# Gathers asked for two experts ahead in a two-layer hybrid trunk, with zero rows written later, products in PSUM, one more 2 KB slot and an earlier split of the last share

## The chip, the cores and the metric

The kernel runs on one core of one Trainium2 chip. Five engines work side by side, each through its own instruction stream: TensorE (PE, matmuls; PEld is its weight load), VectorE (DVE), ScalarE (ACT), GpSimd (POOL) and SyncE (SP). They wait for each other through semaphores. [...] The metric is device microseconds of the whole program; lower is better. SBUF, the on-chip memory, has 128 partitions; PSUM, where matmuls write, has eight banks of 2 KB for each partition.

## The reference

512 tokens of 1024 values pass two layers. Each layer is a mixer and then a mixture of experts, each with a residual and a layer norm:

```python
for layer in range(2):
    m = conv_mixer(x, ...) if layer == 0 else rglru_mixer(x, ...)
    x = layer_norm(ALPHA * x + m, ln1_g[layer], ln1_b[layer])
    f = moe(x, w_router, b_router, moe_w1[layer], moe_w3[layer], moe_w2[layer])
    x = layer_norm(ALPHA * x + f, ln2_g[layer], ln2_b[layer])

# moe: a router picks one group of four experts, and in it two of them, for each token
hb = silu(xb @ w1[e]) * (xb @ w3[e])     # xb: the tokens that chose expert e
y  = hb @ w2[e]                          # 1024 x 1024 weights, float32, 16 experts
out[token] += gate * y
```

The mixer of layer 0 is an input projection to 2560 columns, a causal convolution of 31 taps with GLU, norm and swish on one half, a gated short convolution on the other, and an output projection. That of layer 1 is a gated linear recurrence.

## The kernel before

**Precision.** A float32 product runs as three passes: a weight tile `raw` is split into `wh` (rounded to fp32r by ACT, line L137) and `wl` (the remainder, subtracted by DVE or POOL, L148). Experts with few tokens (places `SMALL` = 2, 5, 8, 11 and 13 of the 16) are packed as half rows and multiply `raw` directly (class `Small`, matmuls L226); the others are blocks of up to 128 tokens (class `Block`, matmuls L305, gate product L326).

**The weight stream.** Class `Stream` loads all weights in a fixed order through SP's queue (L121): 1 MB for an expert's tile and 12 tiles for an expert (four units each of w1, w3 and w2), 512 KB for a tile of the mixers. A load waits until a slot of the `V8` or `V` pool is free; `ws.lead` says how many tiles are split ahead of their use, `ws.cap` how much may be held.

**Layer 0's mixer.** `conv_mixer` goes through 20 column tiles of the projection (PE L596 to L599). ACT evicts each (L800), splits the next weight tile (L137) and makes taps (L767, L772); DVE does most of the convolution's taps (L761), POOL some of the rest (L773) and weight subtracts. At each tile a `hook(idx)` is called. At `idx` 3 it builds constants on POOL and makes the generator `dram_rows`, which then advances one step with every tile: a POOL memset of a tile `zero` (L1059) and ten DMAs on ACT's queue that write it to DRAM (one of 0.5 MB at L1064 and four of 1 MB at L1068 for each layer), where it is the starting value of the rows into which the experts' results are scattered and of the rows that padding gathers.

**Routing.** `route` (L1115) computes places on DVE with narrow tiles of the small pool; `by_place` (L1243) reorders by a masked product `perm` of 128x1024 in a `V` slot and a sum (L1248, L1249), twice in a layer. The first expert's matmuls stand beside it on PE.

**The experts.** `moe` (L1345) takes the 16 places in order. In iteration `e` (current expert `cur`, next `nxt`) POOL first gathers the rows of expert `e + 1` by an indirect DMA into the one buffer `rows` (`gather`, L1325). Then PE does w1 and w3 of `cur`, each in four units (0 to 3). After `w3(2)`, `nxt.rows_in(xe)` transposes the gathered rows on PE (L271), which reads the buffer; then come `w3(3)`, the transposes of the hidden values (L215 in a small expert), the first unit `w1(0)` of `nxt`, and w2 of `cur`. At the end of the iteration ACT evicts y, and POOL scatters it to DRAM with an indirect DMA (`scatter`, L1340). So POOL's queue holds the scatter of `e - 1` right in front of the gather of `e + 1`.

```python
xe = self.gather(slots[e + 1], e + 1 in SMALL, rows)   # start of iteration e
...
cur.w3(2)
nxt.rows_in(xe)
```

**The last expert.** Its y is not scattered. `share(h)` scales one half of it (DVE, L1493), `total_mm(t, h)` adds it to token tile t on PE (L1499), `total_half(t, h)` folds the result into the sum `az` (DVE, L1506, L1507).

Of the kernel before, what the change touches and what calls it, by code (L numbers as in the profile page):

```python
# [11 lines left out]
F32 = mybir.dt.float32  # L12
F32R = mybir.dt.float32r
BF = mybir.dt.bfloat16
I32 = mybir.dt.int32
AF = mybir.ActivationFunctionType
OP = mybir.AluOpType
AX = mybir.AxisListType

P = 128  # L20
T = 512
NT = T // P
D = 1024
KD = D // P
HALF = 512
E = 16
# [3 lines left out]
ALPHA = 4.0 ** 0.25  # L30
LRU_C = 8.0
NV = 21
NW = 11

# [1 line left out]
SMALL = (2, 5, 8, 11, 13)  # L38
# [309 lines left out]
class Trunk:  # L348
# [766 lines left out]
    def route(self, meanwhile):  # L1115
        nc, v = self.nc, self.nc.vector
        G4 = NT * NG

        def s(w, dt=F32):

            return self.S([P, G4, w], dt, f"rt{w}{'b' if dt == BF else ''}", bufs=2 if w == 2 or dt == BF else 4)

        def b(ap, n):
            return ap.broadcast_to([P, ap.shape[1], n])

        def tg(ap):
            return ap.rearrange("p (t g) o -> p t (g o)", g=NG)

        desc = self.desc[:, None, 0:EPG]
        lg = self.logit.rearrange("p t (g e) -> p (t g) e", g=NG)  # L1130

        l = s(2)
        v.tensor_reduce(l[:, :, 0:1], lg, axis=AX.X, op=OP.max)
        e1, e2, f, lm = s(4), s(4), s(4), s(4)
        v.tensor_tensor(e1, lg, b(l[:, :, 0:1], EPG), op=OP.is_equal)
        top = self.S([P, NT, 1], F32, "top", bufs=2)
        v.tensor_reduce(top, l[:, :, 0].rearrange("p (t g) -> p t g", g=NG), axis=AX.X, op=OP.max)
        v.tensor_tensor(f, e1, desc.broadcast_to([P, G4, EPG]), op=OP.mult)
        q1, q2 = s(1), s(1)
        v.tensor_reduce(q1, f, axis=AX.X, op=OP.max)  # L1140
        v.tensor_tensor(e1, f, b(q1, EPG), op=OP.is_equal)
        v.scalar_tensor_tensor(lm, e1, -1e30, lg, op0=OP.mult, op1=OP.add)
        v.tensor_reduce(l[:, :, 1:2], lm, axis=AX.X, op=OP.max)

        d, r = s(2), s(2)
        topb = top.broadcast_to([P, NT, NG])
        for i in range(2):
            v.tensor_tensor(tg(d[:, :, i:i + 1]), tg(l[:, :, i:i + 1]), topb, op=OP.subtract)
        nc.scalar.activation(d, d, AF.Tanh, scale=0.5)
        meanwhile()  # L1150
        v.tensor_tensor(e2, lm, b(l[:, :, 1:2], EPG), op=OP.is_equal)
        v.tensor_tensor(f, e2, desc.broadcast_to([P, G4, EPG]), op=OP.mult)
        v.tensor_scalar(r, d, -1.0, 1.0, op0=OP.mult, op1=OP.add)
        v.reciprocal(r, r)
        v.scalar_tensor_tensor(d, d, 1.0, r, op0=OP.add, op1=OP.mult)
        v.tensor_reduce(q2, f, axis=AX.X, op=OP.max)

        gs, ge = s(1), s(1)
        v.tensor_tensor(gs, d[:, :, 0:1], d[:, :, 1:2], op=OP.add)
        v.tensor_tensor(e2, f, b(q2, EPG), op=OP.is_equal)  # L1160
        gm = self.S([P, NT, 2], F32, "gm", bufs=2)
        v.tensor_reduce(gm[:, :, 0:1], tg(gs), axis=AX.X, op=OP.max)
        v.tensor_tensor(f, e1, e2, op=OP.add)
        v.tensor_tensor(tg(ge), tg(gs), gm[:, :, 0:1].broadcast_to([P, NT, NG]), op=OP.is_equal)
        v.tensor_tensor(tg(ge), tg(ge), self.desc[:, None, 0:NG].broadcast_to([P, NT, NG]), op=OP.mult)
        v.tensor_reduce(gm[:, :, 1:2], tg(ge), axis=AX.X, op=OP.max)
        v.tensor_tensor(tg(ge), tg(ge), gm[:, :, 1:2].broadcast_to([P, NT, NG]), op=OP.is_equal)
        ab = s(4, BF)
        v.tensor_tensor(ab, f, b(ge, EPG), op=OP.mult)
        ab = ab.rearrange("p (t g) e -> p t (g e)", g=NG)  # L1170

        ps = self.bank([P, 2, NT, E])
        nc.tensor.matmul(ps[:, 0], self.tri, ab, start=True, stop=False)
        for t in range(1, NT):
            nc.tensor.matmul(ps[:, 0, t:], self.ones, ab[:, 0:NT - t], start=False, stop=(t == NT - 1))
        for t in range(NT):
            nc.tensor.matmul(ps[:, 1, 0], self.ones, ab[:, t], start=(t == 0), stop=(t == NT - 1))
        self.pos = self.S([P, NT, E], F32, "pos", bufs=1)
        v.scalar_tensor_tensor(self.pos, ps[:, 0], 1.0, ab, op0=OP.add, op1=OP.mult)
        self.cnt_ps = ps  # L1180
        self.gate_parts = (e1, e2, d, gs, ge)
# [61 lines left out]
    def by_place(self, dst, src):  # L1243

        v = self.nc.vector
        n = [P, NT, E, E]
        w = self.V(n, F32, "perm")
        v.tensor_tensor(w, src[:, :, None].broadcast_to(n), self.sel[:, None].broadcast_to(n), op=OP.mult)  # L1248
        v.tensor_reduce(dst, w, axis=AX.X, op=OP.add)  # L1249

    def extra_blocks(self):

# [92 lines left out]
    def moe(self, layer, loaded):  # L1345

        nc, tc, ws = self.nc, self.tc, self.ws
        v = nc.vector
        slots, hot = {}, []
# [9 lines left out]
        rows = self.R("in", "xe")  # L1359
        nc.gpsimd.memset(rows, 0.0)  # L1360
        xe = self.gather((first[0][:, 0:1],), False, rows)
# [15 lines left out]
        slots[0], = self.slot_rows([hot0], [aux(0)], [False], first)  # L1377
        fill([1, 2, 3], hot)
        hot = []
        for e in range(E):  # L1380
            cur, last = nxt, e == E - 1
            if not last:
                xe = self.gather(slots[e + 1], e + 1 in SMALL, rows)
            if e < 12:
                q = e // 4 * 4 + 4 + 2 * (e % 4)
                if e % 4 < 2:
                    hot += [self.one_hot(self.pos[:, :, i], nc.gpsimd, i in SMALL) for i in (q, q + 1)]
                if e % 4 == 2:
                    q = e // 4 * 4 + 4
                    fill(list(range(q, q + 4)), hot)  # L1390
                    hot = []
            if e == E - 2:
                ws.cap = 16
            if e:
                cur.w1(1)
                cur.w1(2)
                if last:
                    self.base_begin()
                cur.w1(3)
            cur.w3(0)  # L1400
            if e == 1:
                self.extra_blocks()
            if e == 4:
                self.nextra = nc.values_load(self.ni[0:1, 0:1], min_val=0, max_val=32)
            cur.w3(1)
            cur.w3(2)
            if not last:
                nxt = Small(self, ws) if e + 1 in SMALL else Block(self, ws, 4 if e == E - 2 else 2)
                nxt.rows_in(xe)
            ws.later = []  # L1410
            cur.w3(3)
            cur.turn(0)
            ws.lows()
            if last:
                cur.turn(1)
            else:
                nxt.w1(0, ws.next(), lambda h: h or cur.turn(1))
                ws.ahead()
            cur.w2(0)
            if last:  # L1420
                loaded()
                self.base_sum(0)
            cur.w2(1)
            if e == E - 2:
                self.place_rows(slots[E - 1][0])
            if last:
                break
            cur.w2(2)
            cur.w2(3)
            self.scatter(cur.ys, slots.pop(e), cur.small, ROOM[e])  # L1430
            if e == E - 2:
                with tc.If(self.nextra > 0):  # L1432
                    it = self.S([P, 1], F32, "it", bufs=1)
                    nc.vector.memset(it, 0.0)
                    self.kept = {}
                    with tc.For_i(0, self.nextra, 1):
                        self.extra(layer, it)
                    self.kept = None
# [8 lines left out]
        for t in range(NT):  # L1447
            self.total_mm(t, 0)
        cur.w2(3)
        for t in range(NT):  # L1450
            self.total_half(t, 0)
        self.share(1, cur.ys[1], gate)
        for t in range(NT):
            self.total_mm(t, 1)
        ws.total, ws.open, ws.cap = False, False, 10
        ws.lead = 4
# [115 lines left out]
def build(ctx, tc, I, out, dbg=None, stop=None):  # L1572
# [43 lines left out]
    steps, rows = [], []  # L1616

    def hook(idx):
        if idx == 1:
            k.channel_params(*rows0, prm)  # L1620
        if idx == 2:
            ws.low(nc.gpsimd)
            ws.cap = 18
        if idx == 3:
            k.consts()
            rows.append(k.dram_rows())
        if rows:
            next(rows[0], None)
        if idx == 5:
            k.channel_params(*rows1, prm1)  # L1630
            steps.append(k.router_weights(prm1[:, :, 10:11], prm1[:, :, 12:13]))
            next(steps[0])
        if idx in (8, 10):
            next(steps[0])
            ws.lead = 3
        if idx == 12:
            ws.lead = 2
            ws.low(nc.gpsimd, nc.vector)
        if idx == 14:
            ws.cap = 10  # L1640
        if idx == 19:
            ws.lead = 0

    k.conv_mixer(xT, first, prm, hook)
    xT = None
    g1 = k.bcast_rows(I["ln1_g"][0], "g1")
# [146 lines left out]
```

## Time and profile before

| | us |
|---|---|
| median of 3 runs | 1580.95 (1580.26 to 1586.53) |
| the profiled execution, its own time | 1580.28 |
| its span, first to last instruction | 1578.4 |
| PE busy in the span | 1411.9 |
| DVE busy in the span | 1124.9 |
| ACT busy, POOL busy | 772.8, 425.2 |

All times of the rows below are in microseconds from the span's start unless marked ns. A row of a timeline gives start, duration, engine, line and operation, output tile and input tiles, and in brackets how long the engine sat idle before it and what released it. The engines' busy time is of instructions; a matmul's record ends by a model, later than the next one starts. The granted clock of TensorE is given as a share of full speed. The stages are: layer 0's mixer to about 190 us, its routing to about 240, its experts to about 740, layer 1's mixer to about 960, its routing to about 1017, its experts to about 1540.

### The profile page before, as it was taken

What the parts mean: (1) busy time and instruction counts of PE and PEld (TensorE: products, weight loads), DVE (VectorE), ACT (ScalarE), POOL (GpSimd) and SP (SyncE); (2) the same over time, 40 slices, a digit from 0 to 9 for tenths busy, and PEclk for the clock granted to TensorE, in tenths of its full rate; (3) what the DMA queues carried; (4) which work ended last, traced back from release to release, by engine and by line L of the source; (5) the groups of instructions that cost most, each with busy time, mean ns of one, the idle gap of its engine ahead of it and who ended that gap; (6) DMA issues with size and microseconds to landing.
All of it is one profiled execution on the core that took longest, in us unless ns stands there. A gap on an engine that the chain in (4) does not pass through costs nothing. (4 is left out here: it accounts for less than half of the span.)

```text
span 1578.4 us, 18166 instructions
## 1 busy us (share of the span) xinstructions
PE 1411.9 (89%) x6456; PEld 1031.1 (65%) x6456; DVE 1124.9 (71%) x1234; ACT 772.8 (49%) x718; POOL 425.2 (27%) x370
## 2 busy tenths in 40 slices
PE   8898969999899998999589798699998999989982
PEld 7686738567486674667477677484775847755761
DVE  6798688568384683558989987884855848644786
ACT  3543227357374573457455421363755637543751
POOL 3783114104201401002473311240051014100043
PEclk9999979999999999999789899799999999999996
DMA  9833747999999999978922258499999999999681
GB/s 283 334 134 107 269 188 300 386 417 380 410 392 392 422 390 418 395 290 323 269 82 84 102 196 310 151 364 403 397 397 417 386 408 399 393 419 399 249 327 53
DMA packets 120838, 490.71 MB, mean 311 GB/s; under 512 B 14079, under 2 KB 53503, under 8 KB 70565
## 3 DMA queue, kind: packets, MB, share of 16 engines
q1 hardware_dynamic: 102240, 437.29, 71.4%
q0 software_dynamic: 11808, 35.28, 5.7%
q10 hardware_dynamic: 6692, 16.91, 2.8%
q8 instruction: 53, 0.87, 0.2%
q14 instruction: 45, 0.36, 0.1%
HBM read 469.50 MB, written 29.62 MB: 316 GB/s over the span
## 5 line engine op out<-in xcount | busy, mean ns | idle before, releaser
L148 DVE TENSOR_TENSOR wl<-raw,wh 128x2048 fp32r<-128x2048 f32 (+2 forms) x310 | 628.2, 2069 | 239.5 <-ACT wh L137 226.1
L137 ACT ACTIVATE wh<-raw 128x2048 fp32r<-128x2048 f32 (+1 forms) x312 | 535.0, 1757 | 113.2 <-PE p L305 19.2
L305 PE MATMUL p<-wh,xe 128*128 128x512 f32 x1344 | 346.5, 395 | 0.8 <-PEq L1432 0.6
L305 PEld LDWEIGHTS p<-wh,xe 128*128 128x128 f32 x1344 | 247.9, 188 | 56.2 <-issue 7.0
L1340 POOL DMA_INDIRECT yd<-y,io x30 | 31.3, 1044 | 772.6 <-DVE wl L148 321.5
L305 PE MATMUL p<-wl,xe 128*128 128x512 f32 x672 | 187.3, 390 | 2.4 <-DVE wl L148 2.4
L226 PE MATMUL b<-raw,xs 128*64 128x512 f32 x640 | 154.2, 626 | 0.0
L305 PEld LDWEIGHTS p<-wl,xe 128*128 128x128 f32 x672 | 125.8, 188 | 31.2 <-DVE wl L148 4.1
L596 PE MATMUL b<-xT,wh 128*128 128x512 f32 (+1 forms) x320 | 120.3, 382 | 13.2 <-ACT wh L137 13.2
L1272 POOL TENSOR_SCALAR S<-c,posp 128x128 bf16<-128x128 bf16 x96 | 124.9, 1314 | 0.5
L597 PE MATMUL b<-xT,wh 128*128 128x512 f32 (+1 forms) x320 | 119.0, 378 | 2.7 <-DVE xT L421 2.7
L226 PEld LDWEIGHTS b<-raw,xs 128*64 128x64 f32 x640 | 44.4, 144 | 81.4 <-issue 78.7
L148 POOL TENSOR_TENSOR wl<-raw,wh 128x1024 fp32r<-128x1024 f32 x28 | 71.9, 2574 | 37.6 <-ACT wh L137 37.6
L596 PEld LDWEIGHTS b<-xT,wh 128*128 128x128 f32 x320 | 62.6, 196 | 26.0 <-ACT wh L137 15.8
L599 PE MATMUL b<-xT,wl 128*128 128x512 f32 (+1 forms) x320 | 72.9, 371 | 2.0 <-DVE wl L148 2.0
L271 PE MATMUL b<-c,xe 128*128 128x128 f32 x176 | 31.4, 334 | 45.5 <-DMA xe<-x1d,ii 45.5
L597 PEld LDWEIGHTS b<-xT,wh 128*128 128x128 f32 x320 | 62.6, 196 | 13.5 <-DVE xT L421 3.2
L226 PE MATMUL b<-raw,hts 128*64 128x512 f32 x320 | 70.9, 595 | 0.0
L418 ACT ACTIVATE xe<-b 128x512 fp32r<-128x512 f32 x40 | 22.6, 596 | 92.6 <-PE b L271 92.5
L599 PEld LDWEIGHTS b<-xT,wl 128*128 128x128 f32 x320 | 56.8, 191 | 12.4 <-DVE wl L148 2.5
L421 DVE TENSOR_TENSOR xe<-b,xe 128x512 fp32r<-128x512 f32 x40 | 26.5, 686 | 53.1 <-ACT xe L418 53.0
L271 PEld LDWEIGHTS b<-c,xe 128*128 128x128 f32 x176 | 27.1, 212 | 55.2 <-DMA xe<-x1d,ii 41.0
(309 smaller groups left out, 1961.2 us busy)
## 6 DMA issues: line engine op xcount, KB each, us to landing
raw<-in_moe_w_dram SPq DMA_DIRECT2D x384, 1024.0 KB, 9.9
raw<-in_even_w_in_dram SPq DMA_DIRECT2D x20, 512.0 KB, 8.0
yd<-zero ACTq DMA_DIRECT2D x8, 1024.0 KB, 8.2
ay<-yd POOLq DMA_DIRECT2D x8, 1024.0 KB, 15.4
raw<-in_odd_w_in_dram SPq DMA_DIRECT2D x16, 512.0 KB, 7.1
raw<-in_even_w_out_dram SPq DMA_DIRECT2D x8, 512.0 KB, 8.9
x1d<-z POOLq DMA_DIRECT2D x8, 512.0 KB, 6.2
az<-x1d POOLq DMA_DIRECT2D x8, 512.0 KB, 12.4
```

Of the source, the lines that this page charges most:

```text
L137: self.k.nc.scalar.activation(wh, raw, AF.Copy)
L148: self.lo[0].tensor_tensor(wl, raw, wh.bitcast(F32), op=OP.subtract)
L226: self.nc.tensor.matmul(ps[64 * h:64 * h + 64], stat[i], w[0][:, i, h * HALF:(h + 1) * HALF], start=(first and i == 0), stop=(last and i = ...
L271: self.nc.tensor.transpose(ps[:, q], v[:, q // step, q % step], self.k.ident)
L305: self.nc.tensor.matmul(pss[j], stat[i][a], q[:, i, j * HALF:(j + 1) * HALF], start=(first and i == 0 and a == 0 and q is wh), stop=(last ...
L418: self.nc.scalar.activation(hi, src, AF.Copy)
L421: self.nc.vector.tensor_tensor(lo, src, hi.bitcast(F32), op=OP.subtract)
L596: nc.tensor.matmul(ps, ah, bh, start=(i == 0), stop=False)
L597: nc.tensor.matmul(ps, ah, bl, start=False, stop=False)
L599: nc.tensor.matmul(ps, al, bh, start=False, stop=(i == n - 1))
L1272: (eng or self.nc.vector).tensor_scalar(S[:, t], self.iota2 if small else self.iota, pos[:, t:t + 1], None, op0=OP.is_equal)
L1340: nc.gpsimd.indirect_dma_start(out=self.by_half(self.yd) if small else self.yd[:, :], out_offset=bass.IndirectOffsetOnAxis(ap=slot[2], axi ...
```

## The change

There are five edits. The gather of expert 1 is issued before the loop, and within iteration `e` the gather of expert `e + 2` right after `rows_in` of expert `e + 1`, so it stands in POOL's queue ahead of the scatter of `e`. `by_place` makes its product in two halves of 128x512 in PSUM banks, where it used one 128x1024 tile of SBUF. The generator of zero rows first advances at column tile index 10, so its memset and ten DMAs fall to indices 10 to 19. The pool of 2 KB slots has 12 where it had 11, and the narrow tiles of `route` are cut from one of them. At the end of the experts, `share(1)` comes after the first two `total_half`, and the other two alternate with their `total_mm`.

```diff
-NW = 11
+NW = 12
@@ route
+        cols, at = self.W([P, HALF], F32, "rt"), [0]
         def s(w, dt=F32):
-            return self.S([P, G4, w], dt, f"rt{w}{'b' if dt == BF else ''}", bufs=2 if w == 2 or dt == BF else 4)
+            if dt == BF:
+                return self.S([P, G4, w], dt, "rtb", bufs=1)
+            at[0] += G4 * w
+            return cols[:, at[0] - G4 * w:at[0]].rearrange("p (n w) -> p n w", w=w)
@@ by_place
-        n = [P, NT, E, E]
-        w = self.V(n, F32, "perm")
-        v.tensor_tensor(w, src[:, :, None].broadcast_to(n), self.sel[:, None].broadcast_to(n), op=OP.mult)
-        v.tensor_reduce(dst, w, axis=AX.X, op=OP.add)
+        n = [P, NT // 2, E, E]
+        for c in (slice(0, NT // 2), slice(NT // 2, NT)):
+            w = self.bank().rearrange("p (t q e) -> p t q e", t=NT // 2, q=E)
+            v.tensor_tensor(w, src[:, c, None].broadcast_to(n), self.sel[:, None].broadcast_to(n), op=OP.mult)
+            v.tensor_reduce(dst[:, c], w, axis=AX.X, op=OP.add)
@@ moe
+        xe = self.gather(slots[1], 1 in SMALL, rows)
         for e in range(E):
             cur, last = nxt, e == E - 1
-            if not last:
-                xe = self.gather(slots[e + 1], e + 1 in SMALL, rows)
...
                 nxt.rows_in(xe)
+                if e + 2 < E:
+                    xe = self.gather(slots[e + 2], e + 2 in SMALL, rows)
...
-        for t in range(NT):
+        for t in range(2):
             self.total_half(t, 0)
         self.share(1, cur.ys[1], gate)
-        for t in range(NT):
+        for t in range(2):
+            self.total_mm(t, 1)
+        for t in range(2, NT):
+            self.total_half(t, 0)
             self.total_mm(t, 1)
@@ hook
-        if rows:
+        if rows and idx >= 10:
             next(rows[0], None)
```

## Rows read from the trace of the kernel before

**Rows 1.** The page's head: the span, the busy time of each engine with its share of the span and its instructions, and the granted clock of TensorE in 40 equal slices, in tenths of full speed.

```profile
span 1578.4 us, 18166 instructions
PE 1411.9 (89%) x6456; PEld 1031.1 (65%) x6456; DVE 1124.9 (71%) x1234; ACT 772.8 (49%) x718; POOL 425.2 (27%) x370
PEclk9999979999999999999789899799999999999996
```

**Rows 2.** The waits of PE in 240 to 740 us (layer 0's experts, the first row) and in 1030 to 1540 us (layer 1's, the second row): total us, times, longest.

```profile
PE b L271 <- DMA xe<-x1d,ii: 16.3, 5, 4.1
...
PE b L271 <- DMA xe<-x1d,ii: 15.9, 5, 3.7
```

**Rows 3.** The timeline of PE around two small experts of layer 0: expert 2 (the first four rows) and expert 13 (the last four). Each begins with the six units w1(1) to w3(2) as one run of 48 matmuls.

```profile
301.16 10.52 PE L226 MATMUL b<-raw,xs 128*64 128x512 f32 x48
315.04 1.98 PE L271 MATMUL b<-c,xe 128*128 128x128 f32 x8 [3.36 <-DMA xe<-x1d,ii]
...
320.26 0.75 PE L215 MATMUL b<-c,hs 128*128 128x128 f32 x4 [0.80 <-DVE hs L245]
320.76 1.17 PE L305 MATMUL p<-wh,xe 128*128 128x512 f32 x4
...
661.09 10.52 PE L226 MATMUL b<-raw,xs 128*64 128x512 f32 x48
674.53 1.22 PE L271 MATMUL b<-c,xe 128*128 128x128 f32 x8 [2.92 <-DMA xe<-x1d,ii]
...
678.41 0.75 PE L215 MATMUL b<-c,hs 128*128 128x128 f32 x4 [0.79 <-DVE hs L245]
678.91 1.17 PE L305 MATMUL p<-wh,xe 128*128 128x512 f32 x4
```

**Rows 4.** Windows: their bounds and length, then busy time (instructions) of PE, PEld, DVE, ACT and POOL, the granted clock, the DMA share and GB/s. The first two rows and the sum are of ten windows, one for each small expert of both layers, from the end of its run of 48 matmuls to the first matmul of the next expert. The row behind the sum is the part of expert 13's window from the start of its transposes.

```profile
311.68:320.76 9.08, 4.92 (x21) 2.77 (x21) 2.07 (x3) 1.20 (x2) 0.00 (x0) 0.81 1.02 423
...
671.60:678.91 7.31, 3.60 (x21) 2.02 (x21) 1.98 (x3) 1.08 (x2) 0.00 (x0) 1.00 1.02 425
...
sum 88.37, PE 48.13 PEld 24.67 DVE 20.53 ACT 11.73 POOL 0.17; mean PE 4.81 PEld 2.47 DVE 2.05 ACT 1.17 POOL 0.02
...
674.53:678.91 4.38, 3.59 (x20) 2.02 (x21) 1.98 (x3) 1.08 (x2) 0.00 (x0) 1.00 1.02 425
```

**Rows 5.** The timeline of POOL at the start of expert 2, and the gathers among the DMA issues (count, median us from issue to landing).

```profile
302.20 1.07 POOL L1340 DMA_INDIRECT yd<-y,io  x1 [20.26 <-ACT y L1338]
303.57 1.05 POOL L1325 DMA_INDIRECT xe<-x1d,ii  x1 [0.31 <-issue]
...
xe<-x1d,ii POOLq DMA_INDIRECT x32, 9.2
```

**Rows 6.** The waits of SP's weight queue in 240 to 740 us (total, times, longest), and windows, with the columns of rows 4, over the blocks and small experts of layer 0, of layer 1, and of one stretch of blocks alone.

```profile
SPq L121 <- DVE wl L148: 193.5, 71, 20.3
SPq L121 <- PE p L305: 90.6, 51, 7.8
...
300.00:690.00 390.00, 369.67 (x1705) 247.17 (x1704) 233.50 (x176) 206.68 (x167) 65.40 (x57) 0.98 1.00 403
1078.00:1470.00 392.00, 372.09 (x1713) 248.53 (x1712) 233.95 (x177) 208.64 (x168) 67.05 (x58) 0.98 0.99 403
330.00:390.00 60.00, 60.00 (x275) 48.12 (x272) 48.52 (x32) 43.00 (x34) 17.91 (x12) 1.00 0.99 396
```

**Rows 7.** Layer 0's mixer: timelines of ACT (three rows), POOL and PE, a wait of DVE in 24 to 215 us (total, times, longest), and windows with the columns of rows 4.

```profile
41.41 1.06 ACT L137 ACTIVATE wh<-raw 128x1024 fp32r<-128x1024 f32 x1 [14.24 <-DMA raw<-in_even_w_out_dram]
...
57.41 1.06 ACT L137 ACTIVATE wh<-raw 128x1024 fp32r<-128x1024 f32 x1 [9.50 <-DMA raw<-in_even_w_in_dram]
...
124.24 0.70 ACT L772 ACTIVATE ctmp<-av,c 128x485 f32<-128x485 f32 x1 [8.19 <-DVE by L813]
...
37.68 2.06 POOL L1059 MEMSET zero<- 128x2048 f32 x1
...
58.52 0.63 PE L596 MATMUL b<-xT,wh 128*128 128x512 f32 x1 [4.84 <-ACT wh L137]
...
DVE av L801 <- ACT av L800: 9.0, 2, 5.9
...
60.00:145.00 85.00, 78.06 (x335) 63.53 (x335) 83.05 (x112) 36.78 (x51) 62.91 (x39) 0.97 0.46 169
20.00:60.00 40.00, 34.30 (x170) 28.64 (x169) 24.76 (x45) 9.95 (x14) 17.16 (x45) 0.98 1.09 337
75.00:135.00 60.00, 53.06 (x227) 42.91 (x225) 58.98 (x77) 23.59 (x33) 46.02 (x29) 0.97 0.26 92
```

**Rows 8.** The two operations of `by_place` (min, median and max ns, first and last start), the gate product of a block from PSUM (count, busy us and mean ns, then idle time before it), and the timeline of DVE behind the first routing.

```profile
L1248 DVE TENSOR_TENSOR perm<-pos,sel x2: 1224/1225/1226, 220.4 to 997.3; 128x1024 f32<-128x1024 f32 x2
L1249 DVE TENSOR_REDUCE posp<-perm x2: 1220/1220/1220, 221.6 to 998.5; 128x64 f32<-128x1024 f32 x2
...
L326 DVE TENSOR_TENSOR hs<-hs,p 128x512 f32<-128x512 f32 x44 | 30.2, 686 | 38.1 <-PE p L305 38.0
...
239.28 0.16 DVE L1307 TENSOR_REDUCE sg<-b 128x1 f32<-128x3 f32 x1 [2.27 <-PE b L1286]
```

**Rows 9.** The timeline of DVE at the second half of the last share, in layer 0 and in layer 1.

```profile
770.79 0.69 DVE L1506 TENSOR_TENSOR az<-az,b 128x512 f32<-128x512 f32 x1 [0.59 <-PE b L1499]
...
1550.24 0.69 DVE L1506 TENSOR_TENSOR az<-az,b 128x512 f32<-128x512 f32 x1 [0.60 <-PE b L1499]
```

## The prediction

> **What bounds the kernel now.** The first view is the page's head: PE is busy for 1411.9 of 1578.4 us, DVE for 1124.9, and the granted clock is at full speed in most slices [rows 1]. So PE is the first suspect, but the share is a mean over stages, and what counts is what ends PE's waits in each. The second view is therefore PE's waits in the two expert stages, which fill about 1000 us. One line stands out: PE waits for the gathered rows at L271, 16.3 us in five waits in layer 0 and 15.9 us in five in layer 1 [rows 2]. The third view, PE's timeline, tells where these five are. Expert 2, a small one, begins with a run of 48 matmuls that lasts 10.52 us; then PE stands still for 3.36 us until its successor's rows have landed, and the eight transposes that follow take 1.98 us where those of expert 13 take 1.22 [rows 3]. The windows give the reason: in expert 2's stretch the granted clock is 0.81, in expert 13's it is 1.00 [rows 4]. The reader is to see that the wait costs more than its own length where the clock falls to its lower level, 1.2 GHz, behind the standstill.
>
> Why is the gather late? On POOL it is issued at 303.57, behind the scatter at 302.20, so 2.4 us after expert 2's first matmul at 301.16, and a gather takes 9.2 us to land [rows 3, 5]. That sum is more than the 10.52 us of work in front of the transposes. A block has more work there, and only small experts show the wait.
>
> The second candidate in the expert stages is the weight stream: 403 GB/s over both layers' stretches with a DMA share of 0.99 to 1.00 [rows 6]. But its queue on SP waits for slots, 193.5 us for those that DVE frees and 90.6 us for PE's, up to 20.3 us at a time [rows 6]. A queue that waits for slots is ahead of its users; PE has no wait for a weight of that size [rows 2]. So PE bounds these stages, and 60 us of blocks run without a gap [rows 6].
>
> In layer 0's mixer it is different. From 60 to 145 us DVE is busy for 83.05 of 85 us, PE for 78.06 [rows 7]: DVE is the bound there. Ahead of it ACT is held twice, 14.24 us until 41.41 and 9.50 us until 57.41. ACT's queue has the DMAs of zero rows in it, the first of which needs the memset that POOL makes only at 37.68; and with the zero rows the DMA engines are full (share 1.09 in 20 to 60 us) [rows 7]. DVE waits 9.0 us for ACT's evictions in two waits, and PE 4.84 us in one [rows 7].
>
> **Part 1, the gathers.** Nothing is added: the same gathers, one place earlier. Issued when the transposes of e + 1 have read the buffer, the gather of e + 2 has the rest of expert e (w3(3), w1(0) of the next and w2) and six units of expert e + 1 in front of its use. The six units alone last 10.52 us even in a small expert, and a landing takes 9.2 [rows 3, 5]. So all ten waits go. What POOL now waits for, the transposes, is over before the scatter of e behind it has its input: the scatter in the timeline waited 20.26 us for ACT's y [rows 5]. Nothing else that PE needs soon stands there, so I cost that at 0.
>
> The saving: the ten windows from the end of a run of 48 to the next expert's first matmul sum to 88.37 us [rows 4]. With rows present such a window is what expert 13's is from its transposes on, 4.38 us at clock 1.00 [rows 4]. Ten are 43.8, so 44.6 us go. That leaves out that a matmul's record ends after its successor starts: the four transposes at 320.26 end at 321.01, the next matmul starts at 320.76, 0.25 us earlier [rows 3]. Ten such overlaps are 2.5 us. I take 44.6 + 2.5 = 47, with 44.6 and 49.5 (twice the overlap) as bounds if the rows are there. The transposes of the hidden values still wait 0.8 us each for DVE [rows 3]; that is what is late next.
>
> Can the weights follow? Each layer's stretch of 390 us must become 23.5 shorter, which asks for 403 x 390 / 366.5 = 429 GB/s if nothing is drawn from what is held. In the stalls the stream ran at 423 to 425 [rows 4]. At 425 the stretch can be 390 x (1 - 403/425) = 20.2 us shorter by rate alone; the other 3.3 us must come from weights held ahead, and the waits for slots of up to 20.3 us [rows 6] say they are there. I take no loss. The Trainium skill (DMA: Bandwidth & Descriptors, Specifications) gives about 358 GB/s as the limit of HBM for one core, which would make the weights the bound already and the gathers' removal worth nothing: about 1572 us. Here the stream holds 403 GB/s over 390 us and 425 in a window, so the trace does not agree, and I follow the trace.
>
> **Part 2, `by_place` in PSUM.** Removed are a product of 1.22 us and a sum of 1.22 us for each call, added two of each on half the size. A row with a PSUM operand of 128x512 is the gate product, 0.69 us [rows 8]: 4 x 0.69 = 2.76 against 2.44, so +0.3 a call, +0.6 a routing, +1.3 in all. Behind the calls DVE sits idle for 2.27 us until PE is done [rows 8], which covers 0.6. I take 0; uncovered it is +1.3. The freed 8 KB slot lets weight loads start earlier, which is worth nothing while weights are ahead.
>
> **Part 3, the zero rows later.** The same memset and ten DMAs, from the eleventh column tile on. What goes is ACT's wait at 41 us for the memset and its wait in 48 to 57 us in a full DMA system. On DVE, the later bound, that is the 9.0 us it waited [rows 7]. What comes: the memset of 2.06 us now stands in a POOL that is busy for 46.02 of 60 us (75 to 135), and ACT waits for it with its DMA; the transfers themselves fall where the DMA share is 0.26 [rows 7], so they collide with little. Bounds: 0, if ACT is held there as long as it was; 9.0 + 2.06 = 11, if the memset also slowed others and no longer does. I take 9.0 - 2.06 = 7.
>
> **Part 4, a twelfth slot, `route`'s columns in one.** No instruction is added. ACT was held once for 8.19 us by such a slot [rows 7], in the stretch where DVE is the bound; I take 0, at most 5.
>
> **Part 5, the last share.** `share(1)` earlier lets PE's second half start while DVE does the first tiles; DVE's waits for PE of 0.59 and 0.60 us [rows 9] go: 1.2 us. Lower bound 0, if the scaling only delays the sums by as much.
>
> **Sum.** 47 + 7 + 1.2 = 55.2. The profiled execution took 1580.3 us, 1.9 more than its span, which stays; the median of the runs is 0.7 above it. 1580.3 - 55.2 = 1525.
>
> **Rivals.** *The weight stream becomes the bound* (0.12): for it speaks a DMA share of 1.00 [rows 6], against it the waits for slots. If it can't exceed its mean rate, parts 3 and 5 remain, 1580.3 - 8.2 = 1572; with 425 GB/s and no stock, 2 x 20.2 replace the 47, 1532. Its middle is 1552. *ACT is held at the eleventh tile as it was at the fourth* (0.10): the busy POOL speaks for it, the light DMA against it; 1580.3 - 48.2 = 1532. *The gathers come no earlier* (0.05), since POOL is held by something that the trace of before doesn't show at that place: 1572. *Slower* (0.05): without its ten rests PE is granted a lower clock in the experts. PE is busy there for 369.67 + 372.09 = 742 us at a mean clock of 0.98 [rows 6]; at clock c they become 742 x 0.98/c. That eats the 55.2 and 7.9 more at c = 0.90; at 0.85 it is +111 and the time 1636. Against it: 60 us without a gap at clock 1.00 [rows 6]; the lower clock came behind rests [rows 4]. The Trainium skill (TensorE: Matmul & The Clock Gate, Part 1) knows a reduced clock under load once three cores of a die are busy and says that one core never trips it; the trace, with one core, agrees as far as its 60 us at 1.00 go.
>
> **Numbers.** The forecast has 0.68. Its own range: 44.6 alone gives 1536, 49.5 + 11 + 1.2 + 5 gives 1514. The range of 8 in 10 takes in half of the weight stream's case, 1512 to 1550. A measurement of this kernel can tell about 0.5%, 7.9 us, from no change. Faster: the forecast, the held ACT, and the first rival and the third but for their parts at 1572, together 0.90. Within 0.5%: these parts, 0.05. Slower: 0.05.
>
> **What would show it.** Right: no wait of PE at L271 for the gathered rows in either expert stage, a window of 4 to 4.5 us at clock 1.00 in each small expert, and a stretch of about 366 us at over 420 GB/s with few waits for weights; ACT without its holds at 41 and 57 us; DVE's wait for PE gone in the last share. Wrong: waits of PE or DVE for a raw weight or for `wl` in the later experts (first rival); ACT idle for over 5 us around 75 to 100 us in front of its DMA (second); a gather issued on POOL well behind the transposes (third); a granted clock under 0.95 in a stretch without rests (last).

## The result and the profile after

The changed kernel takes 1525.98 us, the median of three runs (1523.43 to 1530.19), and the ratio to the kernel before is 0.9646 (95% interval 0.9598 to 0.9694). Forecast was 1525 us. The profile shown is of the slowest of the three, 1530.19 us; a second one, of a later run with a span of 1524.2 us, stands beside it where the two differ.

The page's head, the lines that answer to [rows 1]:

```profile
span 1528.4 us, 18167 instructions
PE 1396.3 (91%) x6456; PEld 1026.4 (67%) x6456; DVE 1126.9 (74%) x1242; ACT 772.2 (51%) x718; POOL 432.9 (28%) x370
PEclk9999979999999999999799999799999999999995
```

PE has the same 6456 matmuls, and its busy time is 15.6 us less. About 13 of these lie in the ten windows of [rows 4], where eight had a granted clock of 0.80 to 0.83: records got shorter since fewer of them ran at the lower clock. The eight more instructions of DVE are the halves of `by_place`.

The waits of PE in layer 0's experts, 235 to 715 us, all that the trace shows, and the three largest of layer 1's, 980 to 1490 us (total, times, longest), answering to [rows 2]:

```profile
PE b L215 <- DVE hs L245: 4.0, 5, 0.9
PE p L305 <- DVE wl L148: 0.9, 2, 0.5
PE p L305 <- PEq L1439: 0.8, 1, 0.8
...
PE b L1509 <- DVE yl L1503: 5.5, 1, 5.5
PE b L215 <- DVE hs L245: 4.0, 5, 0.9
PE p L305 <- DVE wl L148: 2.5, 2, 1.9
```

The wait at L271 for gathered rows is gone from both. In the whole trace two such waits are left, 13.9 us, for the first expert's rows in the routing; these two stood before as well, with 13.3 us. PE's timeline around expert 2, answering to [rows 3], and POOL's around the same expert, answering to [rows 5]:

```profile
292.54 10.52 PE L226 MATMUL b<-raw,xs 128*64 128x512 f32 x48
302.99 1.23 PE L271 MATMUL b<-c,xe 128*128 128x128 f32 x8
304.14 1.94 PE L226 MATMUL b<-raw,xs 128*64 128x512 f32 x8
306.87 0.74 PE L215 MATMUL b<-c,hs 128*128 128x128 f32 x4 [0.79 <-DVE hs L245]
```

```profile
274.72 2.01 POOL L1331 DMA_INDIRECT xe<-x1d,ii  x1 [1.44 <-PE b L215]
293.57 1.01 POOL L1346 DMA_INDIRECT yd<-y,io  x1 [16.84 <-DVE su L1303]
304.49 1.01 POOL L1331 DMA_INDIRECT xe<-x1d,ii  x1 [9.91 <-PE b L271]
318.41 1.03 POOL L1346 DMA_INDIRECT yd<-y,io  x1 [12.91 <-DVE wl L148]
```

The gather for expert 3's rows is issued at 274.72, 28.3 us ahead of the transposes at 302.99. The next one follows at 304.49, right behind these, and the scatter stands behind it. The eight transposes take 1.23 us, not 1.98: PE no longer rests in front of them.

Windows, with the columns of [rows 4]: nine of the ten stretches between a small expert's run of 48 and the next expert's first matmul (of the tenth the trace shows no single run), first and last and the sum; then the expert stretches, which answer to [rows 6], and the start, which answers to [rows 7]:

```profile
303.06:307.37 4.31, 3.52 (x20) 1.95 (x21) 1.98 (x3) 1.08 (x2) 1.01 (x1) 1.00 1.02 430
...
1398.75:1403.06 4.31, 3.52 (x20) 1.95 (x21) 1.98 (x3) 1.08 (x2) 1.02 (x1) 1.00 1.01 420
sum 38.89, PE 31.70 PEld 17.55 DVE 17.78 ACT 9.77 POOL 9.44; mean PE 3.52 PEld 1.95 DVE 1.98 ACT 1.09 POOL 1.05
```

```profile
291.00:657.00 366.00, 361.98 (x1700) 244.13 (x1700) 231.70 (x176) 205.29 (x165) 66.08 (x56) 1.00 1.01 418
1046.00:1413.00 367.00, 362.97 (x1703) 244.36 (x1701) 232.41 (x176) 205.29 (x165) 66.05 (x56) 1.00 1.01 418
...
20.00:60.00 40.00, 40.00 (x199) 33.90 (x198) 33.71 (x59) 16.11 (x22) 23.80 (x50) 1.00 1.07 314
60.00:135.00 75.00, 70.51 (x303) 57.59 (x303) 71.81 (x96) 31.61 (x43) 56.48 (x34) 0.95 0.45 167
```

A stretch now lasts 38.89 / 9 = 4.32 us where it lasted 8.84 [rows 4]. Over a whole stretch of experts the clock is 1.00, and the DMA engines move 418 GB/s, where they moved 403 [rows 6]. This is all traffic: in 291 to 657 us 152.99 MB, of which SP's weight queue has 146.15 and the gathers and scatters 6.53.

Where the 50.0 us between the two profiled spans went, by PE's stage marks (end of the last matmul of layer 0's projection; first and last block matmul of each expert stage; end):

```
                                before    after   second profile of after
layer 0's projection             140.7    130.9    131.5
routing, first expert             98.7    100.0    101.0
layer 0's experts                527.4    504.7    504.4
share, layer 1's mixer, routing  250.6    250.3    249.9
layer 1's experts                527.7    510.2    504.8
last share, norm                  33.3     32.2     32.7
```

Layer 0's mixer and the two expert stages hold all of it; the 5 us between the two profiles of the changed kernel lie in the last expert of layer 1.

### The profile page after: what moved, and what is told of

Read it like the earlier page. It is cut to its first block, busy times and chain, and to the rows that moved or that the text cites. A ratio compares the mean times of both kernels' runs of the same rounds, so it can differ in the third digit from the quotient of the medians.

```text
span 1528.4 us, 18167 instructions
## 1 busy us (share of the span) xinstructions
PE 1396.3 (91%) x6456; PEld 1026.4 (67%) x6456; DVE 1126.9 (74%) x1242; ACT 772.2 (51%) x718; POOL 432.9 (28%) x370
## 5 line engine op out<-in xcount | busy, mean ns | idle before, releaser
L226 PE MATMUL b<-raw,xs 128*64 128x512 f32 x640 | 146.2, 598 | 0.0
L1331 POOL DMA_INDIRECT xe<-x1d,ii x32 | 37.3, 1167 | 291.9 <-PE b L271 138.4
L1344 ACT ACTIVATE y<-p,sg 128x512 f32<-128x512 f32 x40 | 25.3, 685 | 75.4 <-PE p L305 75.4
L761 DVE SCALAR_TENSOR_TENSOR b<-av,c,b 128x510 f32<-128x510 f32 (+27 forms) x87 | 59.8, 731 | 2.2 <-ACT b L754 1.3
L326 DVE TENSOR_TENSOR hs<-hs,p 128x512 f32<-128x512 f32 x44 | 30.2, 685 | 39.6 <-PE p L305 39.6
```

The costliest lines, as they stand in the source:

```text
L226: self.nc.tensor.matmul(ps[64 * h:64 * h + 64], stat[i], w[0][:, i, h * HALF:(h + 1) * HALF], start=(first and i == 0), stop=(last and i = ...
L326: self.nc.vector.tensor_tensor(self.hm[h], self.hm[h], self.p3[h], op=OP.mult)
L761: nc.vector.scalar_tensor_tensor(o[:, s:], av[:, 0:T - s], prm[:, i, 30 - s:31 - s], acc[:, s:], op0=OP.mult, op1=OP.add)
L1331: self.nc.gpsimd.indirect_dma_start(out=xe, out_offset=None, in_=self.by_half(self.x1d) if small else self.x1d[:, :], in_offset=bass.Indir ...
```

## The experiments

Each ratio is to the kernel before on the same chip. The experiments ran on three chips, so small differences from the changed kernel are judged by the ratios; its own, run again, is 0.9665 (0.9644 to 0.9686).

**The changed kernel again.**

> The changed kernel itself, so that what is compared with it has its time from the same chip. All theories expect about 0.965 of the kernel before, 1526 us, and the stage times of its first profile within 2 us: about 131 us for the end of layer 0's projection, 508 and 514 us for the two expert stages.

Measured: 1525.95 us (1525.35 to 1530.88, five runs). The projection ends at 131.5 us and the expert stages take 504.4 and 504.8 us. The total is as expected. Counted to the end of the last share, as the expectation did, the stages are 507.8 and 508.7 us: layer 1's is 5 us shorter than expected from the first profile. That is a spread between executions of the same kernel, and it lies in that stage's last expert.

**The gathers back.** Theory against a rival that gives the gain to the slots.

```diff
-        xe = self.gather(slots[1], 1 in SMALL, rows)
         for e in range(E):
             cur, last = nxt, e == E - 1
+            if not last:
+                xe = self.gather(slots[e + 1], e + 1 in SMALL, rows)
...
-                if e + 2 < E:
-                    xe = self.gather(slots[e + 2], e + 2 in SMALL, rows)
```

> The changed kernel with the gather of expert e + 1 issued at the start of iteration e again; the other four edits stay. My theory: the ten waits at L271 come back with their half clock, 47 us, so about 1573 us, and the expert stages are 23 us longer each. Rival, that the gain in the experts came from the freed slots and the twelfth 2 KB slot through the weight stream: 1526 us to 1535 us, with the expert stages as short as in the changed kernel.

Measured: 1568.82 us, ratio 0.9931 (0.9911 to 0.9951), 42.9 us above the changed kernel. Its expert stages take 526.2 and 527.4 us. The waits of PE in layer 0's experts and the timeline at expert 2:

```profile
PE b L271 <- DMA xe<-x1d,ii: 15.9, 5, 3.5
...
305.03 1.98 PE L271 MATMUL b<-c,xe 128*128 128x128 f32 x8 [3.51 <-DMA xe<-x1d,ii]
306.94 2.74 PE L226 MATMUL b<-raw,xs 128*64 128x512 f32 x8
```

All of it is back, and the eight transposes take 1.98 us again. With the slots in place and the gathers late the experts gain 1.2 us at most; the rival falls.

**The gathers alone**, on the kernel before.

```diff
+        xe = self.gather(slots[1], 1 in SMALL, rows)
         for e in range(E):
             cur, last = nxt, e == E - 1
-            if not last:
-                xe = self.gather(slots[e + 1], e + 1 in SMALL, rows)
...
+                if e + 2 < E:
+                    xe = self.gather(slots[e + 2], e + 2 in SMALL, rows)
```

> The kernel before with part 1 alone. My theory, that the parts add up: what the changed kernel lost when it was undone there, 43 us, so about 1538 us, with no wait at L271 in the experts but the first. Rival, that the gathers need the freed slots to pay: less than 35 us, over 1546 us, with waits for weights in the later experts.

Measured: 1535.01 us, ratio 0.9711 (0.9691 to 0.9730), 46.2 us below the kernel before. The expert stages take 502.8 and 504.8 us, and the longest wait for a split in them is 1.2 us. The gathers need nothing else of the change.

**The gather in front of the scatter.** What made the gather late, its line in the program or its place in POOL's queue?

```diff
                 nxt.rows_in(xe)
-                if e + 2 < E:
-                    xe = self.gather(slots[e + 2], e + 2 in SMALL, rows)
...
             cur.w2(3)
+            if e + 2 < E:
+                xe = self.gather(slots[e + 2], e + 2 in SMALL, rows)
             self.scatter(cur.ys, slots.pop(e), cur.small, ROOM[e])
```

> The changed kernel with the gather of expert e + 2 moved down in the program, from behind rows_in to the line right in front of the scatter of expert e. In POOL's queue it still stands ahead of that scatter. My theory, that what held the gather was its place behind the scatter, which waits for ACT's y: 1526 us as the changed kernel, no wait at L271 in the experts, since POOL has little else to do in between. Rival, that it is the half expert of lead in the program that pays: about half of the 43 us come back, over 1540 us.

Measured: 1524.38 us, ratio 0.9639 (0.9619 to 0.9659). POOL's timeline:

```profile
274.69 2.00 POOL L1331 DMA_INDIRECT xe<-x1d,ii  x1 [1.45 <-PE b L215]
293.52 1.01 POOL L1346 DMA_INDIRECT yd<-y,io  x1 [16.83 <-DVE su L1303]
304.44 1.01 POOL L1331 DMA_INDIRECT xe<-x1d,ii  x1 [9.91 <-PE b L271]
318.36 1.03 POOL L1346 DMA_INDIRECT yd<-y,io  x1 [12.92 <-DVE wl L148]
```

Each issue is within 0.05 us of the changed kernel's. So the edit is, in what POOL sees, an exchange of two neighbours. POOL holds a DMA until its input is there, and what stands behind it waits as well: before, the gather stood behind a scatter that waited 20.26 us for ACT's y and was issued 0.31 us after it [rows 5]; now it stands ahead of it. That the program asks for the rows half an expert earlier has no part in it.

**The zero rows early again.**

```diff
-        if rows and idx >= 10:
+        if rows:
             next(rows[0], None)
```

> The changed kernel with the zero rows from column tile 3 again. My theory: the first stage gets its two holds of ACT back and is 7 to 9 us longer, about 1534 us, with the rest unchanged. Rival, that the 9 us of the first stage came from the twelfth 2 KB slot, not from the zero rows: 1526 us with the projection's end near 131 us.

Measured: 1533.26 us, ratio 0.9701 (0.9680 to 0.9721), 7.3 us above the changed kernel; the projection ends at 140.4 us, 8.9 later than in the changed kernel's second profile. ACT's timeline and a wait of DVE in 20 to 200 us:

```profile
41.35 1.06 ACT L137 ACTIVATE wh<-raw 128x1024 fp32r<-128x1024 f32 x1 [14.12 <-DMA raw<-in_even_w_out_dram]
57.37 1.06 ACT L137 ACTIVATE wh<-raw 128x1024 fp32r<-128x1024 f32 x1 [9.51 <-DMA raw<-in_even_w_in_dram]
...
DVE av L801 <- ACT av L800: 8.9, 2, 6.0
```

Both holds of ACT and DVE's wait are back as in [rows 7]. The gain of the first stage belongs to the zero rows.

**The memset early.** In the changed kernel ACT is held at the new place as well, and PE waits later on; the two rows of its timelines:

```profile
78.94 1.06 ACT L137 ACTIVATE wh<-raw 128x1024 fp32r<-128x1024 f32 x1 [11.71 <-POOL zero L1059]
...
117.16 0.79 PE L596 MATMUL b<-xT,wh 128*128 128x512 f32 x1 [3.96 <-ACT wh L137]
```

The experiment makes the memset at tile 4 and leaves the DMAs:

```diff
         nc.gpsimd.memset(zero, 0.0)
         self.rows = []
+        yield
...
-        if rows and idx >= 10:
+        if rows and (idx == 4 or idx >= 10):
             next(rows[0], None)
```

> The changed kernel with the memset of the zero tile at column tile 4, its ten DMAs still from tile 10. In the changed kernel ACT is held 11.71 us until 78.94 behind that memset in POOL's queue. Theory, DVE bounds that stretch and covers the hold: no change, 1525 to 1527 us, with ACT's hold gone and the projection's end still near 131 us. Rival, the hold is what PE's later wait of 3.96 us at 117 us comes from: 4 us shorter, 1522 us.

Measured: 1526.77 us, ratio 0.9658 (0.9634 to 0.9683). The hold of 11.71 us is gone, PE still waits 4.0 us once for ACT's split, so that wait doesn't come from the hold, and the projection ends at 129.3 us. A gain of 1 to 2 us there would not show in the total; the rival's 4 us are not there. DVE, busy for 71.81 of the 75 us from 60 to 135, covers the hold.

**The slots back**, parts 2 and 4 undone together (11 slots, `perm` in an 8 KB slot, the routing's tiles in the small pool).

```diff
-NW = 12
+NW = 11
...
-        for c in (slice(0, NT // 2), slice(NT // 2, NT)):
-            w = self.bank().rearrange("p (t q e) -> p t q e", t=NT // 2, q=E)
...
+        w = self.V(n, F32, "perm")
...
```

> The changed kernel with parts 2 and 4 undone: the product of by_place in one 8 KB slot, 11 slots of 2 KB, the narrow tiles of the routing in the small pool. By the prediction, which gave both parts nothing: 1526 us, within 0.3 us for the routing. Rival, that a slot more brings the weight stream ahead or frees ACT in layer 0's mixer: 2 to 5 us longer, 1528 to 1531 us.

Measured: 1527.29 us, ratio 0.9662 (0.9643 to 0.9681): not to be told from the changed kernel's 0.9665. The projection ends at 133.4 us, some 2 us later than with twelve slots, the routing stage and the experts are the same. ACT's hold that the prediction laid to a slot (8.19 us in [rows 7]) and the wait of PE behind it go with these 2 us; first the changed kernel's ACT, then ACT and PE with the slots back:

```profile
115.46 0.70 ACT L772 ACTIVATE ctmp<-av,c 128x484 f32<-128x484 f32 x1 [7.58 <-DVE by L813]
...
116.59 0.70 ACT L772 ACTIVATE ctmp<-av,c 128x485 f32<-128x485 f32 x1 [12.39 <-DVE by L813]
...
119.64 0.79 PE L596 MATMUL b<-xT,wh 128*128 128x512 f32 x1 [6.29 <-ACT wh L137]
```

The twelfth slot makes the hold 4.8 us shorter and PE's wait 2.3 (6.29 to 3.96), but doesn't end either. Parts 2 and 4 are worth 0 to 2 us. The two operations of `by_place` in the changed kernel, in PSUM (min, median and max ns, first and last start), answer to [rows 8]:

```profile
L1254 DVE TENSOR_TENSOR b<-pos,sel x2: 687/694/701, 211.3 to 212.6; 128x512 f32<-128x512 f32 x2
L1255 DVE TENSOR_REDUCE posp<-b x2: 690/690/691, 212.0 to 213.3; 128x32 f32<-128x512 f32 x2
```

**The last share as before.**

```diff
-        for t in range(2):
+        for t in range(NT):
             self.total_half(t, 0)
         self.share(1, cur.ys[1], gate)
-        for t in range(2):
-            self.total_mm(t, 1)
-        for t in range(2, NT):
-            self.total_half(t, 0)
+        for t in range(NT):
             self.total_mm(t, 1)
```

> The changed kernel with the last share split as before. By the prediction, which gave the new order 1.2 us: 1.2 us longer, about 1527 us. By the changed kernel's trace, where DVE waits 2.17 us for the last w2 with only two sums in front of it in layer 1: 1 to 2 us shorter, about 1524.5 us. Both are under what the times tell apart, so the windows from the last matmul of w2 to the last sum decide.

Measured: 1526.38 us, ratio 0.9653 (0.9636 to 0.9670), no difference in the total. DVE's timeline in layer 1 of the changed kernel's first profile:

```profile
1488.63 3.48 DVE L1496 SCALAR_TENSOR_TENSOR az<-az,ay 128x1024 f32<-128x1024 f32 x3
...
1496.93 0.75 DVE L1503 SCALAR_TENSOR_TENSOR yl<-p,sg,yh 128x512 fp32r<-128x512 f32 x1 [2.17 <-ACT yh L1502]
1497.59 0.68 DVE L1516 TENSOR_TENSOR az<-az,b 128x512 f32<-128x512 f32 x1
```

and of the kernel with the old order:

```profile
1489.89 3.48 DVE L1493 SCALAR_TENSOR_TENSOR az<-az,ay 128x1024 f32<-128x1024 f32 x3
...
1498.56 0.73 DVE L1500 SCALAR_TENSOR_TENSOR yl<-p,sg,yh 128x512 fp32r<-128x512 f32 x1
1499.88 0.69 DVE L1513 TENSOR_TENSOR az<-az,b 128x512 f32<-128x512 f32 x1 [0.59 <-PE b L1506]
```

The new order takes the wait of 0.59 us away as forecast, but in this pair it puts one of 2.17 in its place: with two sums instead of four ahead of it, DVE comes to `share(1)` before PE has finished w2. From the first `yl` to the end the new order then takes 1528.4 - 1487.97 = 40.43 us, the old 1528.1 - 1489.23 = 38.87. In the second profile of the changed kernel, where DVE comes later, `share(1)` waits for nothing and the same stretch is 1524.2 - 1484.51 = 39.69, against 1578.4 - 1538.05 = 40.35 in the kernel before. So in these two pairs of profiles the part gains 0.7 us once and loses 1.6 once, by how DVE and PE happen to meet.

**The second pass left out.** How near is the weight stream?

```diff
-        steps = [(a, q, i, j) for a, q in ((0, wh), (1, wh), (0, wl)) for i in range(n) for j in range(len(pss))]
+        steps = [(a, q, i, j) for a, q in ((0, wh), (0, wl)) for i in range(n) for j in range(len(pss))]
...
-            if after is not None and c % (3 * n) == 3 * n - 1:
+            if after is not None and c % (2 * n) == 2 * n - 1:
```

> The changed kernel, with the second of the three passes of the block experts left out (the remainder of the rows times the rounded weights), so a third of their matmuls on PE; all loads, splits and other work stay. It asks how far the weight stream is from being the bound. In the changed kernel a weight lands 13 us before its use in the later experts, at 418 GB/s. Theory, the stream is the next bound: each expert stage gets only 15 to 40 us shorter, 1445 to 1495 us in all, with PE waiting for raw weights, or for splits behind them. Rival, PE stays the bound: 1536 matmuls of 0.227 us in a layer, a third of that is 116 us, so about 1295 us.

Measured: 1521.21 us, ratio 0.9625 (0.9602 to 0.9649). A third of the blocks' matmuls is gone and the time falls by 5 us only; the expert stages take 500.4 and 503.7 us. This is far above both expectations. A window, the longest waits of SP's weight queue in 291 to 657 us, of ACT and DVE in the same stretch, and of PE in 235 to 700 us:

```profile
291.00:657.00 366.00, 319.58 (x1370) 185.49 (x1367) 236.86 (x174) 210.50 (x170) 74.14 (x58) 0.97 1.01 419
...
SPq L121 <- DMA raw<-in_moe_w_dram: 238.5, 117, 3.1
...
ACT wh L137 <- DMA raw<-in_moe_w_dram: 49.9, 21, 9.3
...
DVE wl L148 <- ACT wh L137: 108.0, 28, 18.4
...
PE p L305 <- DVE wl L148: 22.7, 29, 3.3
```

PE's waits are put down to DVE's splits, but these wait for ACT, and ACT for raw weights. SP's queue, which waited for slots before, now waits for its own earlier loads to land. In this stretch the stream is the bound, at 419 GB/s. How it became so is seen in the time from a weight's landing to the first matmul that reads it, the smallest over the units of an expert of layer 0, worked out from the traces (us):

```
expert                   1     3     6     9    12    14
before                32.3  28.3  27.8  25.8  28.9  26.2
gathers back          34.2  28.6  28.2  28.1  26.6  26.5
changed kernel        32.6  23.0  21.3  18.7  17.7  12.4
turn inside (below)   33.1  22.9  20.2  16.4  14.8   8.8
second pass left out  31.4  18.4   6.8   2.3   2.8   2.6
```

This time is the stock: how far the weights are ahead. Before, it fell by 6 us from expert 1 to 14. In the changed kernel it falls by 20, and without the second pass it is gone by expert 9. So what is left of it, 12 us at expert 14, is the changed kernel's distance from this bound. The trace bears this out: counted from the stage's first block matmul, the last w2 unit of expert 14 starts at 446.4 us without the second pass and at 458.9 in the changed kernel's second profile, 12.5 us apart. The last expert then loses most of that lead, so that a third of the blocks' matmuls, 116 us of PE by the expectation's count, was worth 4.0 and 1.1 us of the two stages. In layer 0's last expert PE waits 6.8 us for ACT's copy of the transposes and 4.1 us for a split; what delays these no run singles out. The rival of that run, that PE stays the bound, falls; its theory had the bound right and the gain, 15 to 40 us a stage, much too high.

**The transposes inside.** The wait at L215 that the prediction called late next:

```diff
-            cur.turn(0)
+            if not cur.small:
+                cur.turn(0)
             ws.lows()
...
-                nxt.w1(0, ws.next(), lambda h: h or cur.turn(1))
+                nxt.w1(0, ws.next(), lambda h: h or cur.turn(int(not cur.small)))
```

> The changed kernel, with the transposes of a small expert's hidden values moved behind the first half of the next expert's w1(0), where a block already has its second half of them. PE's ten waits of 0.8 us at L215 for DVE's product then lie under six matmuls. Theory: up to 8 us shorter, about 1518 us. Rival: w2(0) of the small expert then waits for ACT's copy of the transposes, or the weights can't follow, and nothing is gained, 1526 us.

Measured: 1517.04 us (1512.03 to 1517.43), ratio 0.9586 (0.9566 to 0.9606); the expert stages take 500.5 and 498.8 us. PE's waits in 225 to 720 us, all there are, its timeline at expert 5, and a window:

```profile
PE p L305 <- PEq L1440: 0.7, 1, 0.7
PE p L305 <- DVE wl L148: 0.5, 1, 0.5
...
397.04 1.19 PE L305 MATMUL p<-wh,xe 128*128 128x512 f32 x4
398.07 0.63 PE L305 MATMUL p<-wl,xe 128*128 128x512 f32 x2
398.54 0.63 PE L215 MATMUL b<-c,hs 128*128 128x128 f32 x4
398.92 1.17 PE L305 MATMUL p<-wh,xe 128*128 128x512 f32 x4
...
290.00:650.00 360.00, 360.00 (x1692) 243.19 (x1692) 231.31 (x175) 204.68 (x165) 66.14 (x56) 1.00 1.01 419
```

PE works 360 us without a gap, the DMA engines move 419 GB/s beside it, and the version beats both kernels. It also beats the kernel without the second pass, whose lead is lost in the last expert.

**All three**: the transposes inside, the early memset and the old last share.

> The changed kernel with the transposes of a small expert inside the next expert's w1(0), the early memset and the last share split as before. By the runs with one of these alone, only the first moves the time: 1517 us. If the last share as before or the early memset is worth something beside it, 1513 to 1516 us.

Measured: 1520.10 us (1518.11 to 1524.78), ratio 0.9621 (0.9599 to 0.9643), no better than the transposes alone, by the medians 3 us slower. The expert stages take 501.0 and 504.3 us; the second is 5.5 us longer than with the transposes alone, and all of that lies in its last expert, where two executions of one kernel differed by 5 us too. Neither of the other two is shown to be worth keeping.

## Why the prediction was right

**The bound and the mechanism.** Confirmed from both sides. Ten waits of PE for late rows held the expert stages; taken away they gave 46.2 us alone, put back they cost 42.9, where the forecast was 47. Its working holds in parts: the unhindered stretch, taken from expert 13 as 4.38 us, is 4.32, so ten save 45.2. The 2.5 us for overlapping records were too much: with the rows there, the transposes start at 302.99, 0.07 us before the run of 48 ends (292.54 + 10.52), which is 0.7 us for ten, and the 45.2 hold it already. The lower clock went with the rests, as the rows of before said: all nine windows and both expert stretches are at 1.00.

**The weight stream.** Right that it doesn't bind, wrong in the terms: 425 GB/s was read off windows of 7 to 9 us, and over 366 us the DMA engines move 418; the sign of being right "over 420 GB/s" did not come. At 418 the rate alone makes 390 x (1 - 403/418) = 14 us, not 20, and the rest of the 23 came out of the stock, not 3.3 but 9 us by this sum and 14 by the table, of 26. So the rival was nearer than its price said, and the step "a queue that waits for slots is ahead of its users" did not tell how far: in the changed kernel SP's queue still waits 124.6 and 46.0 of 366 us for slots of DVE and PE, the longest 6.1 us. The DMA share of 1.00 that spoke for the rival was the better sign.

**The zero rows.** Forecast 7, undone 7.3. The mechanism differs in one point: the rival that ACT is held at the eleventh tile came true, 11.71 us, and cost next to nothing, since DVE was the bound there and had work. The 2.06 us taken off for the memset were thus not the reason for the size; DVE's wait of 9.0 us was: the projection's end moved by 8.9 us, and where the other 1.6 of it went the runs do not single out. That the term came out at 7 is luck. Nor is the DMA system less full: its share in 20 to 60 us is 1.07 without the zero rows and was 1.09 with them. What changed is who has it: SP's weight queue moves 12.46 MB there and moved 10.83.

**`by_place` and the slots.** Forecast nothing, measured 0 to 2 us. The operations in PSUM take 0.69 us each, as the gate product's row said. The hold of ACT that part 4 was priced by stayed, at 7.58 us for 8.19.

**The last share.** This step failed: 1.2 us forecast, 0.4 measured, which the times can't tell from nothing. It named the wait that goes and not the one that can come, DVE at `share(1)` ahead of PE.

**A slower clock under unbroken work.** It did not come: 360 us without a gap at clock 1.00. Its price at 0.85 was a little low: 742 x 0.98/0.85 is about 113 us more, so about 1638.

The parts add up: 46.2 (alone) + 7.3 (undone) + 1.3 (undone, by times of two chips; the ratios show none) + 0.4 (undone) = 55.2 us, against 55.0 between the medians of the result and 55.5 between those of the second measurement. With the gathers by what they cost when put back it is 51.9. The single terms are uncertain by 2 to 3 us each, so the forecast of 1525 against 1526 is closer than its terms earn.

## What to carry to other kernels

A DMA that waits for nothing can be late because its neighbour in the queue does wait: read the issuing engine's timeline, and exchange the two. A wait that ends in a rest of TensorE is priced by the stretch around it, clock included, against the same stretch where nothing was late. When a bound engine gets faster, ask how much stock the next stream has and at what rate it runs over the whole stretch, since a stall's window shows its best rate, not its mean.

## What the runs showed of the hardware

While the weights stream, the DMA engines move 418 to 419 GB/s over 360 us and more, and no run moves more over such a stretch, whether PE works all the time (the transposes inside) or for 320 of 366 us (the second pass left out). TensorE's granted clock stays at 1.00 for 360 us of unbroken matmuls on one core. And ACT can stand still for 11.71 us in a stretch bound by DVE without the total moving: the ratio is 0.9658 without that hold, 0.9665 with it.
